# Later adaLN vectors summed in 64 pieces of one feature tile instead of 256 quarters

## Chip, cores and metric

One core of one Trainium2 chip runs the kernel. The metric is the device time of one execution in microseconds (us), from the first to the last work on the core. "SP", "PE", "ACT", "DVE" and "POOL" are the five engines: SP issues most DMAs, PE multiplies matrices, ACT, DVE and POOL do the elementwise work.

## The reference, cut to what matters

One layer of a diffusion block on 256 latent tokens and 256 context tokens of 2048 features, in float32. A conditioning vector is turned into six modulation vectors of 2048 features each (adaLN):

```python
def _modulation(cond, w, bias):
    m = jax.nn.silu(cond) @ w + bias          # w: 2048 x 12288
    return [a[:, None, :] for a in jnp.split(m, 6, axis=-1)]
...
o_c, ctx_states = _mix(_modnorm(h_c, norm1_g[l], m_c[0], m_c[1]), h_c.shape[1], zero, lp)
o_x, _ = _mix(_modnorm(h_x, norm1_g[l], m_x[0], m_x[1]), GRID_W, ctx_states, lp)
h_x = h_x + m_x[2] * o_x
h_x = h_x + m_x[5] * _swiglu(_modnorm(h_x, norm2_g[l], m_x[3], m_x[4]), ffn_w_gu[l], ffn_w_down[l])
```

`_mix` projects the modulated tokens with `w_in` (2048 x some 6800), runs four groups of mixers (GLA, Gated DeltaNet, a short gated convolution, RWKV-7; three of them recurrent in both directions, the context first) and projects with `w_out`. The first two vectors (0 and 1) are needed before any projection. The other four (2 and 5, two gates; 3 and 4, shift and scale of the second norm) are needed only after the mixers. These are "the later vectors".

## The kernel before

The kernel runs in stages. From 0 to 190 us it norms the context tokens, computes vectors 0 and 1 (line 391 loads `ada_w` in tiles `ad` of 1 MB, four column strips of PE sum them into `ada`) and projects some context columns (`acc`). From some 199 to 1190 us it runs the mixers of both token sequences, interleaved with the projections that feed them. Then come the output projection with `w_out`, the second norm, and the SwiGLU, whose weights `w_gu` and `w_down` stream through to the end.

All weights are float32 and are cut into two exact halves: a piece is loaded into `wraw`, `split` copies its upper part to `wh` (ACT, line 156) and subtracts for the rest `wl` (DVE, line 161), and PE multiplies with both. Until the SwiGLU, `wraw` is a ring of six buffers of 128 x 512 (256 KB), and `wh` and `wl` have three each (`wp = [wpool, 512, 3, 6]`: pool, width, halves, raw buffers).

`proj` makes 128 projected columns for all tokens. It goes through the 2048 features in four quarters (`hf`); each loads one `wraw` of `w_in` (SP, line 571), splits it, and sums 12 products into the PSUM bank `big` (line 173 is the helper of all matmuls). This is where the later vectors are fed in: `feed` is a list of steps, and each quarter of a projection takes two steps from its head.

The steps come from `ada_pieces`, for the vectors 3, 4, 2 and 5 in turn: 64 steps `piece(j, kt)` and one `finish` each. A step loads 256 KB of `ada_w` into a buffer of the `wraw` ring (SP, line 255): feature tile `kt` (128 features) and from each of the vector's four groups of 512 columns the quarter `j`, 128 columns. Four matmuls follow, one for each group, with the conditioning `sc` as the weights (128 features x 32, of which two columns are used) and the loaded columns streamed; group `g` goes to partitions 32g to 32g+31 of the one bank `ob`. `finish` takes the sums out of `ob`, through a `wraw` buffer.

The whole program is handed to a scheduler that keeps every engine's queue in an order of priority: an instruction's place in the text, save where `tc.high_priority()` puts loads ahead, or where the list `ORDER` names a piece of mixer work with a number after the colon, by which many instructions the piece is put forward or back. SP's queue runs in order: an issue that waits for a buffer holds up those behind it. In `ORDER`, `XX` loads the latents, `FF` takes the steps that are left in `feed`, `YY` closes the pools in `rws` (the RWKV mixers' tiles) to make room for the mixers' outputs. The columns that a mixer needs later are parked in memory through tiles `xs` and fetched again; `put_y` takes a mixer's output from a tile `y_o` (two buffers), the short convolution's from `sc_y` (two of its own).

Of the kernel before, what the change touches and what calls it, by code (L numbers as in the profile page):

```python
# [13 lines left out]
PSUM = bass.MemoryType.PSUM  # L14
# [21 lines left out]
# Order of the work on the two token sequences, lower case for the context and capitals for the latents:  # L36
# pr, pd, pg project and park the inputs of a mixer; rw, gd, gl run one (RWKV pair, GDN head, GLA pair);
# XX loads the latents and their gates, FF finishes the later adaLN vectors, YY makes room for the mixers'
# outputs on chip, SC is a quarter of the short convolution. After a colon: by how many instructions
# a piece is put forward (or back) against its place.  # L40
# [94 lines left out]
def block_kernel(ctx: ExitStack, tc: tile.TileContext, x, cx, ada_w, ada_b, w_in, w_out, w_gu, w_down,  # L135
# [71 lines left out]
    wp = [wpool, 512, 3, 6]  # L207
# [4 lines left out]
    def split(raw, who, pool=None):  # L212
        """raw = h + l exactly, both of a float32r's width"""
        n = 2 if pool else wp[2]
        h = mk(pool or wp[0], [P, wp[1]], "wh", n, F32R)
        l = mk(pool or wp[0], [P, wp[1]], "wl", n, F32R)
        # wide pieces in two steps, for the products to begin on the first
        n = 2 if wp[1] == 1024 else 1
        w = wp[1] // n
        for i in range(n):  # L220
            sl = slice(i * w, (i + 1) * w)
            acopy(h[:, sl], raw[:, sl])
            tt(l[:, sl], raw[:, sl], h.bitcast(F32)[:, sl], SUB, e=who)
        return h, l

    def logsig(o, zin, tmp, lo=0, hi=P, bias=0.0, badd=None):
        """o = log(sigmoid(zin + bias)); tmp is scratch"""
        act(tmp, zin, AF.Abs, bias=bias)
        act(tmp, tmp, AF.Exp, scale=-1.0)
        act(tmp, tmp, AF.Ln, bias=cst["one"][lo:hi])  # L230
        if badd is None:
            stt(o, zin, 0.0, tmp, MIN, SUB)
        else:
            ts(o, zin, badd, ADD, 0.0, MIN)
            tt(o, o, tmp, SUB)
# [6 lines left out]
    gate_dram = mk(dram, [2, D], "gated")  # L242

    def ada_pieces(ci, bank_of, tmp):
        """adaLN columns of one of the later vectors, in steps to be taken between other work"""
        st = {}

        def piece(j, kt):
            if not st:
                st["ps"] = bank_of([P, 512])  # L250
            ps = st["ps"]
            with tc.high_priority():
                raw = wraw()
                rv = raw.rearrange("p (g c) -> p g c", g=4)
                nc.sync.dma_start(rv, ada_w[kt * P:(kt + 1) * P, ci * D:(ci + 1) * D]
                                  .rearrange("p (g c) -> p g c", g=4)[:, :, j * P:(j + 1) * P])
            for g in range(4):
                mm(ps[32 * g:32 * g + 32, j * P:(j + 1) * P], sc[:, kt, :], rv[:, g], kt == 0, kt == KT - 1)
# [22 lines left out]
        return [lambda j=j, kt=kt: piece(j, kt) for j in range(4) for kt in range(KT)] + [finish]  # L281
# [12 lines left out]
    def open_bank(flat):  # L294
        """zeros in a PSUM bank, left open for sums in any order"""
        n = flat.shape[-1]
        mm(flat, zb[:, :P], zb[:, 0:1].to_broadcast([P, n]), True, False)
        return lambda: mm(flat, zb[:, :P], zb[:, 0:1].to_broadcast([P, n]), False, True)
# [3 lines left out]
    C = mk(kp, [P, NCONST], "consts")  # L302
    sw = mk(kp, [P, 1536], "sw")

    def cc(name, n=P):
        return C[:, COFF[name]:COFF[name] + n]

# [9 lines left out]
    # block-diagonal tiles: off-diagonal blocks stay zero  # L317
# [27 lines left out]
    with ExitStack() as st:  # L345
# [41 lines left out]
        def first_vectors(kt):  # L387
            """modulation of feature tile kt, and the modulated context tokens"""
# [52 lines left out]
        for i, dst in ((0, C), (1, sw)):  # L441
            nc.sync.dma_start(dst, (consts, small)[i])
# [20 lines left out]
    def col_products(ps, wh, wl, a, first, last):  # L463
        """ps[:, 0] + ps[:, 1] += w @ a, w and a in exact halves"""
        both = [lambda: mm(ps, wh, a, first, last), lambda: mm(ps[:, 0], wl, a[:, 0], False, False)]
        for f in both[::-1] if last else both:
            f()

    def row_products(acc, aH, aL, wh, wl, first, last, j):
        """acc[j] += a @ w for one half of the tokens; a is stored transposed, both in exact halves"""  # L470
        ah, al = aH[:, j * P:(j + 1) * P], aL[:, j * P:(j + 1) * P]
        mm(acc[j], ah, wh, first, False)
        mm(acc[j], ah, wl, False, False)
        mm(acc[j], al, wh, False, last)

    # ================= mixers =================
    Y = mk(dram, [16, P, T], "Yd")
    with mix:
# [4 lines left out]
        def runsum(o, i, d, z):  # L483
            """running sums, forward or backward, starting anew where z is zero"""
# [12 lines left out]
        # recurrent states at the end of the context, parked  # L497
# [17 lines left out]
        def PB(shape, tag="e"):  # L515
            """a PSUM bank: two for projections, three for either stream of mixers"""
# [3 lines left out]
        def token_scale(ss, tag, tmp):  # L520
            """ss[j]: partial sums of the squares of a token's features -> the norm's factors, [any, tokens]"""
# [40 lines left out]
        def proj(nHL, segs):  # L562
            """w_in columns of segs, transposed: [columns, tokens] in PSUM"""
            H, L = nHL
            ps = PB([P, T], "big")
            for hf in range(4):
# [7 lines left out]
                for f in feed[:2]:  # L574
                    f()
                del feed[:2]
# [14 lines left out]
        def spill(nHL, name, i, s=1):  # L591
            """project columns and park them"""
# [14 lines left out]
        def sigmoid(o):  # L607
            """o = sigmoid(o), o not under -87"""
# [4 lines left out]
        def silu_to(o, z, tag):  # L613
            """o = z * sigmoid(z)"""
# [5 lines left out]
        def inverse(nL, levels, lowers, rhs=None, out=None, w=P):  # L620
            """(I - nL)^-1 for four unit-triangular matrices; lowers says of each if it is a lower one.
            Diagonal blocks of 16 by substitution, then blocks of doubled size.
            With rhs: out = the inverses' transposes times rhs, instead."""
# [5 lines left out]
            # diagonal blocks, one row per partition  # L629
# [5 lines left out]
            # rows r and 15 - r of a block hold 15 entries together; side by side, the second one backwards  # L635
# [8 lines left out]
            # all entries of a block on every partition of that block  # L644
# [7 lines left out]
            for st in range(15):  # L652
                step = []
                for low, us in groups.items():
                    # the entries (i, j) of all j, i the row that is done
# [61 lines left out]
        def smalls(sm):  # L717
            """gate inputs of low rank, and what hangs on them alone"""
            cur[0] = "b"
            # rows 0..15: inputs of the GLA gate; 32..39: running sums of the GDN log decay;  # L720
            # 64..127: shifted RWKV inputs
# [6 lines left out]
            for d in range(2):  # L728
# [7 lines left out]
                # tanh(z) = 2 sigmoid(2 z) - 1  # L736
# [6 lines left out]
            # Gated DeltaNet: log decay, its running sums, beta  # L743
# [4 lines left out]
            # softplus(z) = -logsig(-z)  # L748
# [22 lines left out]
            # sums over whole chunks, on every partition  # L771
# [3 lines left out]
            esel = C[32:40, COFF["esel"]:COFF["esel"] + 32].rearrange("p (r c) -> p r c", c=4)  # L775
            et = mk(mx, [P, 8, 4], "get", 1)
            # rows 0..3 (forward) use the running sum, rows 4..7 (backward) the reversed one
# [19 lines left out]
        def rw_gates(p, d, sm):  # L797
            """sums of sigmoid(.) inside each chunk of 64 (the log decay over -RW_S), and a"""
# [21 lines left out]
        def halves(dst, src, eng):  # L820
            """src [P, 4, 64] -> the diagonal blocks of dst [P, 4, 2, 64]"""
# [18 lines left out]
        def rwkv(p, s, raw, sm):  # L840
# [6 lines left out]
            for d in range(2):  # L847
# [52 lines left out]
                # values, token-major  # L900
# [5 lines left out]
                # L and M  # L906
# [9 lines left out]
                # decayed keys, token-major  # L916
# [5 lines left out]
                # [nB | nA^T]  # L922
# [9 lines left out]
                # [K~ | A_rk^T], token-major  # L932
# [31 lines left out]
                for n, c in enumerate(order):  # L964
                    # [outputs | state]
# [37 lines left out]
        def conv(o, z, taps, s):  # L1003
            """three-tap convolution along rows of 256 (context) or 64 tokens"""
# [9 lines left out]
        def gdn(h, s, raw, sm):  # L1014
# [40 lines left out]
            # decays between tokens; index d * 2 + c  # L1055
# [57 lines left out]
            for d in range(2):  # L1113
                S = get_state(("gd", h, d), f"gd_S{d}") if s == 1 else None
                for n, c in enumerate((0, 1) if d == 0 else (1, 0)):
                    u = d * 2 + c
                    # [outputs | state]
# [33 lines left out]
        def gla(p, s, raw, sm):  # L1151
# [28 lines left out]
            for d in range(2):  # L1180
# [52 lines left out]
                for n, c in enumerate((0, 1, 2, 3) if d == 0 else (3, 2, 1, 0)):  # L1233
                    # [outputs | state]
# [30 lines left out]
        def short_conv(t, nHL):  # L1265
# [6 lines left out]
            yo = t1("sc_y", 2)  # L1272
# [42 lines left out]
        bdE = Ring(rings, "bdE", [P, 4, 2, 64], 1)  # L1315
        for ci in (3, 4, 2, 5):
            feed += ada_pieces(ci, lambda shape: mk(pb, shape, "ob", 1), mx)
# [111 lines left out]
    # ================= SwiGLU =================  # L1429
# [5 lines left out]
    for f in range(FT):  # L1435
        # sums of the products with the tokens' upper parts, and with their lower ones
        pg = [mk(ps2, [P, 2, T], "acc", 8) for _ in range(2)]
        for k0, nk, bufs in ((0, 8, wide), (8, 4, narrow), (12, 4, narrow)) if f == 0 else ((0, 8, wide), (8, 8, wide)):
# [9 lines left out]
            # the first tile takes the tokens as they get ready  # L1448
# [16 lines left out]
    # the table of the last norm's functions, ahead of it  # L1465
# [7 lines left out]
    for b in range(4):  # L1473
# [3 lines left out]
        for k2 in range(FT // 2):  # L1477
            # the last weights of all are kept for the halves of the tokens in turn
# [32 lines left out]
def prepare(inputs):  # L1511
    """host side: arrays as the launch takes them"""
# [24 lines left out]
```

## Time and profile before

| | us |
|---|---|
| median of 3 runs (lowest, highest) | 2065.49 (2064.67, 2066.31) |
| span of the profiled execution | 2059.4 |
| PE busy in that span | 1933.2 (94%) |
| DVE busy, ACT busy | 1341.9 (65%), 988.3 (48%) |
| the later vectors' products (`ob`), PE busy | 110.4 in 2048 records |

The span goes from the first to the last instruction on the core; the runs' median is 6.1 us over it, for what lies around. Matmuls are pipelined and overlap, so the mean duration of one is longer than the time it adds. "Granted clock" is the share of full speed that PE's clock was given. Every float32 matmul shows as two records.

### The profile page before, as it was taken

What the parts mean: (1) busy time and instruction counts of PE and PEld (TensorE: products, weight loads), DVE (VectorE), ACT (ScalarE), POOL (GpSimd) and SP (SyncE); (2) the same over time, 40 slices, a digit from 0 to 9 for tenths busy, and PEclk for the clock granted to TensorE, in tenths of its full rate; (3) what the DMA queues carried; (4) which work ended last, traced back from release to release, by engine and by line L of the source; (5) the groups of instructions that cost most, each with busy time, mean ns of one, the idle gap of its engine ahead of it and who ended that gap; (6) DMA issues with size and microseconds to landing.
All of it is one profiled execution on the core that took longest, in us unless ns stands there. A gap on an engine that the chain in (4) does not pass through costs nothing.

```text
span 2059.4 us, 37523 instructions
## 1 busy us (share of the span) xinstructions
PE 1933.2 (94%) x13864; PEld 1640.5 (80%) x13864; DVE 1341.9 (65%) x3488; ACT 988.3 (48%) x2013; POOL 163.3 (8%) x210
## 2 busy tenths in 40 slices
PE   4777999979999999999999999899999999999998
PEld 2556787758887887888989978788888888888886
DVE  3333875788778957889897776655555555545554
ACT  2112644564456435555654565555555555544444
POOL 0000100000101000101010000200000000000000
PEclk9899999989999999999999999999999999999999
DMA  9997858834847748534333655466666666665554
GB/s 271 277 275 222 240 162 236 228 103 125 227 139 199 204 140 246 136 82 111 102 105 107 166 186 193 135 187 188 187 185 185 188 188 186 185 234 195 193 195 154
DMA packets 609272, 374.31 MB, mean 182 GB/s; under 512 B 31776, under 2 KB 570784, under 8 KB 608192
## 3 DMA queue, kind: packets, MB, share of 16 engines
q1 hardware_dynamic: 604176, 366.59, 61.3%
q10 hardware_dynamic: 4320, 3.15, 0.5%
q8 instruction: 109, 1.79, 0.4%
q0 software_dynamic: 592, 2.18, 0.3%
q14 instruction: 75, 0.61, 0.1%
HBM read 359.89 MB, written 11.94 MB: 181 GB/s over the span
## 4 chain that ended last, share of the span: by engine, by line
PE 73%; DMA 11%; DVE 8%; issue 3%; ACT 2%; POOL 1%; SPq 0%; ACTq 0%; DVEq 0%; POOLq 0%
PE acc L173 36%; PE big L173 14%; PE la L173 8%; DMA ad<-in_ada_w 6%; PE ea L173 4%; PE lb L173 4%; PE ob L173 3%; PE eb L173 3%; DVE wl L161 2%; DMA wraw<-in_w_in 2%; DMA wraw<-in_ada_w 1%; ACT wh L156 1%; DMA wr<-in_w_in 1%; DVE ivaXc L161 1%; DVE ivaw L161 1%
## 5 line engine op out<-in xcount | busy, mean ns | idle before, releaser
L161 DVE TENSOR_TENSOR wl<-wraw,wh 128x512 fp32r<-128x512 f32 x856 | 568.3, 690 | 417.8 <-ACT wh L156 410.0
L156 ACT ACTIVATE wh<-wraw 128x512 fp32r<-128x512 f32 x856 | 509.9, 625 | 544.6 <-PE acc L173 186.2
L173 PE MATMUL acc<-n,wh 128*128 128x512 f32 x1408 | 493.4, 399 | 3.0 <-ACT wh L156 3.0
L173 PE MATMUL acc<-n,wl 128*128 128x256 f32 x1408 | 382.7, 282 | 0.3 <-DVE wl L161 0.3
L173 PE MATMUL big<-nh,wh 128*128 128x256 f32 x1056 | 319.5, 303 | 0.9 <-ACT xs L156 0.9
L173 PE MATMUL big<-nl,wh 128*128 128x256 f32 x1056 | 308.2, 292 | 0.0
L173 PE MATMUL big<-nh,wl 128*128 128x256 f32 x1056 | 306.7, 291 | 1.2 <-DVE wl L161 1.2
L173 PEld LDWEIGHTS acc<-n,wh 128*128 128x128 f32 x1408 | 259.9, 189 | 59.9 <-ACT wh L156 3.3
L173 PEld LDWEIGHTS acc<-n,wl 128*128 128x128 f32 x1408 | 266.9, 190 | 9.3 <-DVE wl L161 0.8
L173 PEld LDWEIGHTS big<-nh,wh 128*128 128x128 f32 x1056 | 199.7, 189 | 29.6 <-issue 23.5
L173 PEld LDWEIGHTS big<-nh,wl 128*128 128x128 f32 x1056 | 199.9, 190 | 8.1 <-issue 5.2
L173 PEld LDWEIGHTS big<-nl,wh 128*128 128x128 f32 x1056 | 199.9, 189 | 7.3 <-issue 6.7
L173 PE MATMUL acc<-wl,hH 128*128 128x512 f32 x352 | 137.1, 389 | 0.0
L173 PE MATMUL acc<-wh,hH 128*128 128x512 f32 x352 | 137.0, 389 | 0.0
L173 PE MATMUL acc<-wh,hL 128*128 128x512 f32 x352 | 137.0, 389 | 0.0
L173 PE MATMUL ob<-wraw,sc 128*32 128x128 f32 x2048 | 110.4, 284 | 10.7 <-DMA wraw<-in_ada_w 7.0
L173 PEld LDWEIGHTS ob<-wraw,sc 128*32 128x32 f32 x2048 | 52.1, 109 | 45.4 <-DMA wraw<-in_ada_w 12.1
L173 PE MATMUL ada<-ad,sc 128*32 128x256 f32 x512 | 46.0, 510 | 37.6 <-DMA ad<-in_ada_w 35.5
L161 POOL TENSOR_TENSOR hL<-sg,hH 128x256 fp32r<-128x256 f32 x44 | 44.5, 1012 | 453.4 <-ACT hH L156 453.4
L173 PEld LDWEIGHTS acc<-wl,hH 128*128 128x128 f32 x352 | 66.1, 188 | 14.2 <-DVE wl L161 0.2
L173 PEld LDWEIGHTS acc<-wh,hH 128*128 128x128 f32 x352 | 66.1, 188 | 13.7
L173 PEld LDWEIGHTS acc<-wh,hL 128*128 128x128 f32 x352 | 66.1, 188 | 13.6
(473 smaller groups left out, 3130.6 us busy)
## 6 DMA issues: line engine op xcount, KB each, us to landing
wraw<-in_w_gu SPq DMA_DIRECT2D x174, 512.0 KB, 4.0
wraw<-in_w_in SPq DMA_DIRECT2D x260, 256.0 KB, 3.0
wraw<-in_ada_w SPq DMA_DIRECT2D x256, 256.0 KB, 3.7
wraw<-in_w_down SPq DMA_DIRECT2D x88, 512.0 KB, 4.3
ad<-in_ada_w SPq DMA_DIRECT2D x32, 1024.0 KB, 8.4
wraw<-in_w_out SPq DMA_DIRECT2D x64, 256.0 KB, 3.2
wr<-in_w_in SPq DMA_DIRECT2D x32, 256.0 KB, 4.0
xin<-in_cx SPq DMA_DIRECT2D x2, 1024.0 KB
```

Of the source, the lines that this page charges most:

```text
L156: A.activation(o, i, AF.Copy)
L161: (e or V).tensor_tensor(out=o, in0=a, in1=b, op=op)
L173: return TE.matmul(o, l, r, start=start, stop=stop)
```

## The change

A step of the later vectors is now a whole feature tile: `piece(kt)` loads 128 features x 2048 columns of a vector (1 MB, rows of 8 KB) into a tile `araw` of its own with one buffer, and four matmuls of 512 columns, one per group, sum it into the same bank. 64 steps and four `finish` in place of 256 and four. A projection takes one step in every second quarter (`hf % 2 == 0`) in place of two in each, the same number of bytes per projection. `araw` lies in `rws`, behind the RWKV mixers' rings. To make room, the `wraw` ring has four buffers in place of six, the constants leave out the identity (which is held elsewhere too), and the short convolution's outputs share the two buffers `y_o`. `ORDER` with its numbers is unchanged. Comments are taken out (not shown).

```diff
-    wp = [wpool, 512, 3, 6]
+    wp = [wpool, 512, 3, 4]
...
+    araw = [None]
+
     def ada_pieces(ci, bank_of, tmp):
         st = {}
 
-        def piece(j, kt):
+        def piece(kt):
             if not st:
                 st["ps"] = bank_of([P, 512])
             ps = st["ps"]
             with tc.high_priority():
-                raw = wraw()
-                rv = raw.rearrange("p (g c) -> p g c", g=4)
-                nc.sync.dma_start(rv, ada_w[kt * P:(kt + 1) * P, ci * D:(ci + 1) * D]
-                                  .rearrange("p (g c) -> p g c", g=4)[:, :, j * P:(j + 1) * P])
+                raw = mk(araw[0], [P, D], "araw", 1)
+                nc.sync.dma_start(raw, ada_w[kt * P:(kt + 1) * P, ci * D:(ci + 1) * D])
             for g in range(4):
-                mm(ps[32 * g:32 * g + 32, j * P:(j + 1) * P], sc[:, kt, :], rv[:, g], kt == 0, kt == KT - 1)
+                mm(ps[32 * g:32 * g + 32, :], sc[:, kt, :], raw[:, g * 512:(g + 1) * 512], kt == 0, kt == KT - 1)
...
-        return [lambda j=j, kt=kt: piece(j, kt) for j in range(4) for kt in range(KT)] + [finish]
+        return [lambda kt=kt: piece(kt) for kt in range(KT)] + [finish]
...
-    C = mk(kp, [P, NCONST], "consts")
+    C = mk(kp, [P, NCONST - P], "consts")
...
-            nc.sync.dma_start(dst, (consts, small)[i])
+            nc.sync.dma_start(dst, (consts[:, P:], small)[i])
...
                     wh, wl = split(raw, V)
-                for f in feed[:2]:
-                    f()
-                del feed[:2]
+                if hf % 2 == 0:
+                    for f in feed[:1]:
+                        f()
+                    del feed[:1]
...
-            yo = t1("sc_y", 2)
+            yo = t1("y_o", 2)
...
         bdE = Ring(rings, "bdE", [P, 4, 2, 64], 1)
+        araw[0] = rws.enter_context(tc.tile_pool(name="araw", bufs=1, reuse_waits="tile"))
         for ci in (3, 4, 2, 5):
             feed += ada_pieces(ci, lambda shape: mk(pb, shape, "ob", 1), mx)
```

## Rows read from the trace of the kernel before

**Rows 1.** The page: span, and the chain that ended last, by engine and by line.

```profile
span 2059.4 us, 37523 instructions
...
PE 73%; DMA 11%; DVE 8%; issue 3%; ACT 2%; POOL 1%; SPq 0%; ACTq 0%; DVEq 0%; POOLq 0%
PE acc L173 36%; PE big L173 14%; PE la L173 8%; DMA ad<-in_ada_w 6%; PE ea L173 4%; PE lb L173 4%; PE ob L173 3%; PE eb L173 3%; DVE wl L161 2%; DMA wraw<-in_w_in 2%; DMA wraw<-in_ada_w 1%; ACT wh L156 1%; DMA wr<-in_w_in 1%; DVE ivaXc L161 1%; DVE ivaw L161 1%
```

**Rows 2.** Windows: busy us (instructions) of each engine, granted clock, DMA share, GB/s.

```profile
199.00:809.00 610.00, 581.03 (x5482) 475.14 (x5486) 462.98 (x1527) 301.32 (x656) 47.90 (x76) 0.98 0.66 187
...
1700.00:2050.00 350.00, 349.60 (x1679) 293.30 (x1678) 187.63 (x301) 165.72 (x312) 21.09 (x18) 1.00 0.60 192
```

**Rows 3.** Windows for tile `ob` alone: PE, PEld, DVE, ACT; sum over 200 to 850.

```profile
200.00:250.00 50.00, 13.33 (x232) 5.86 (x232) 0.00 (x0) 0.00 (x0) 0.97 0.86 242
...
300.00:350.00 50.00, 11.79 (x228) 5.59 (x220) 0.17 (x1) 0.60 (x1) 1.00 0.84 240
350.00:400.00 50.00, 10.79 (x200) 4.88 (x200) 0.00 (x0) 0.00 (x0) 1.00 0.85 234
...
750.00:800.00 50.00, 11.89 (x240) 5.97 (x240) 0.00 (x0) 0.00 (x0) 1.00 0.82 237
...
sum 650.00, PE 111.31 PEld 52.76 DVE 1.70 ACT 1.20; mean PE 8.56 PEld 4.06 DVE 0.13 ACT 0.09
```

**Rows 4.** Waits between 199 and 812 us: us in total, times, longest.

```profile
ACT wh L156 <- DMA wraw<-in_w_in: 80.6, 55, 4.2
...
PE ob L173 <- DMA wraw<-in_ada_w: 7.0, 12, 2.0
```

**Rows 5.** Timeline of PE, four places: start us, us, engine, line, operation.

```profile
59.91 1.93 PE L173 MATMUL ada<-ad,sc 128*32 128x256 f32 x32 [1.83 <-DMA ad<-in_ada_w]
...
204.47 0.28 PE L173 MATMUL big<-nl,wh 128*128 128x256 f32 x1
204.59 0.27 PE L173 MATMUL big<-nh,wl 128*128 128x256 f32 x1
204.79 0.65 PE L173 MATMUL ob<-wraw,sc 128*32 128x128 f32 x16
205.37 0.39 PE L173 MATMUL big<-nh,wh 128*128 128x256 f32 x1
...
400.21 0.43 PE L173 MATMUL ob<-wraw,sc 128*32 128x128 f32 x8
400.57 0.66 PE L173 MATMUL la<-ivaW,ivaL 128*128 128x64 f32 x4
...
420.02 0.97 PE L173 MATMUL la<-ivaR,consts 128*128 128x480 f32 x2
420.82 0.38 PE L551 MATMUL big<-ident,xs 128*128 128x128 f32 x2
```

**Rows 6.** Timeline of PE: the first and the last quarters with others inside.

```profile
207.81 0.42 PE L173 MATMUL ob<-wraw,sc 128*32 128x128 f32 x6
...
208.79 0.62 PE L173 MATMUL ob<-wraw,sc 128*32 128x128 f32 x10
...
808.15 0.43 PE L173 MATMUL ob<-wraw,sc 128*32 128x128 f32 x8
...
808.94 0.64 PE L173 MATMUL ob<-wraw,sc 128*32 128x128 f32 x14
```

**Rows 7.** DMA issues: count, KB each, median us from issue to landing.

```profile
wraw<-in_ada_w SPq DMA_DIRECT2D x256, 256.0 KB, 3.7
...
ad<-in_ada_w SPq DMA_DIRECT2D x32, 1024.0 KB, 8.4
```

**Rows 8.** Waits of SP's queue over the whole span.

```profile
SPq L255 <- PE ob L173: 140.2, 101, 17.7
```

**Rows 9.** Timeline of SP's queue at the start.

```profile
8.31 3.57 SPq L255 DMA_DIRECT2D wraw<-in_ada_w  x2
11.93 0.50 SPq L364 DMA_DIRECT2D xin<-in_cx  x1
```

More of the change, by code (lines that the diff above doesn't have):

```diff
@@ L301, in block_kernel @@
     kp = mix.enter_context(tc.tile_pool(name="kp", bufs=1, reuse_waits="tile"))
-    C = mk(kp, [P, NCONST], "consts")
+    C = mk(kp, [P, NCONST - P], "consts")
     sw = mk(kp, [P, 1536], "sw")
     def cc(name, n=P):
-        return C[:, COFF[name]:COFF[name] + n]
+        return C[:, COFF[name] - P:COFF[name] - P + n]
     lev = {b: cc(f"lev{b}") for b in LEVS}
@@ L774, in smalls @@
                 V.tensor_copy(er[32:40, d, 0:2], smd[d][32:40, (127 if d == 0 else 0):T:P])
-            esel = C[32:40, COFF["esel"]:COFF["esel"] + 32].rearrange("p (r c) -> p r c", c=4)
+            esel = C[32:40, COFF["esel"] - P:COFF["esel"] - P + 32].rearrange("p (r c) -> p r c", c=4)
             et = mk(mx, [P, 8, 4], "get", 1)
```

## Prediction

> **What bounds the kernel now.** I read the page's head and its chain first [rows 1]: the span is 2059.4 us, and PE work carries most of the chain. The quarters themselves (PE `ob`, 3%, some 62 us) and the loads that they wait for (`wraw<-in_ada_w`, 1%, some 20 us) are a small part, so this change moves tens of microseconds at the very most. The windows come next [rows 2]: between 199 and 809 us, the stretch in which the quarters run, PE is busy 581 of 610 us, so only 29 us of it are plain idle, and the DMA engines are at 0.66. PE's program order is what that stretch lasts on; DMA is near its limit in part of it. The same windows for the tile `ob` alone [rows 3] give the object of the change: 111.3 us of PE in 2048 records. A matmul shows as two records, so a quarter (4 matmuls) is 8 records and 0.435 us. They are unevenly spread: the four densest windows hold 232, 228, 200 and 240 records with the DMA share at 0.82 to 0.86. The waits say that PE itself hardly stands for these loads (7.0 us in 12 times), while ACT waits 80.6 us for `w_in` pieces that come on the same queue [rows 4].
>
> **The products.** What one quarter costs beyond its columns is seen in the order of time [rows 5]. The matmuls of a quarter go to four column strips and run side by side. A single quarter takes from 400.21 to 400.57, 0.36 us; two in a row from 204.79 to 205.37, 0.58 us; so a further quarter costs 0.22 us and each unbroken group some 0.14 us on top. Going in costs as well: the products before follow each other at 0.12 us, the group starts 0.20 us after the last, so 0.08 us per entry. For the new shape the nearest row is `ada`, the same four strips with 256 columns: 32 records in 1.93 us at full clock, 4 groups of four. A new piece is one group of four with 512 columns, as many columns as half of that: 0.96 us. 64 of them are 61.5 us in place of 111.3.
>
> That holds while the four stay together. They often don't: in the timeline I followed the 256 quarters, and they stand in 208 groups with 55 places where other products stand inside a quarter (the first and the last of them, groups of 6 + 10 and of 8 + 14 records, stand in [rows 6]). 42 of the 55 breaks come right after a quarter's first matmul. A broken piece loses the strips' overlap, since a lone matmul streams all its columns by itself. The price of a lone one comes from the 480-column product [rows 5], 420.02 to 420.82: 0.80 us, so 0.85 us for 512 columns, about 1.0 with the group's own 0.14. How many of the new pieces break isn't in the trace. Lower bound: 55 in 256, 14 of 64. Upper bound: breaks follow columns, which stay the same in sum, 55. The breaks after the first matmul come with a slot (two quarters per slot before, one piece after, so at most 42 in 128, 21 of 64), the other 13 with the time that the products take. I take the middle of 14 and 42, 28: 28 us.
>
> So PE for the vectors goes from 111.3 to 61.5 + 28 = 89.5 us, 22 less, and with 92 groups in place of 208 there are 116 x 0.08 = 9 us less of entries: 31 us. All of it is in a stretch where PE is busy throughout, but freed PE time shortens a kernel only where the chain runs over PE. By the chain of the page that is 73%: 23 us.
>
> **The loads.** 256 loads of 256 KB become 64 of 1 MB, rows of 8 KB in place of four runs of 512 B. In the feed stretch 512-byte runs move 187 GB/s at a share of 0.66, 283 GB/s for a full engine set; the `w_down` stage, 2 KB runs, 192 at 0.60, 320 GB/s [rows 2]. 67 MB at 320 in place of 283 are 27 us less of DMA time, which nothing on the chain waits for directly: I count none of it. SP has 192 fewer loads to issue.
>
> What it adds is the wait on a single buffer. Load n+1 is issued when piece n's last matmul is done, so from one piece to the next pass at least a landing and a piece. Landing of 1 MB: below, 256 KB land in 3.7 us [rows 7], of which 0.93 are bytes at 283 GB/s, leaving 2.8, and 1 MB at 320 GB/s takes 3.3, so 6.1 us as an estimate; above, the 1 MB row, 8.4 us, taken with the DMA engines full and two such loads together. The pieces' own spacing: 610/64 = 9.5 us on average, where even 8.4 + 1.0 just fits. In the four dense windows, 900 records are 28 pieces in 200 us, 7.1 us each. 6.1 + 1.0 = 7.1 fits to the hair; 9.4 misses by 2.3 us, 64 us over 28 pieces. I take 0.4 us each, 11 us, near the lower end, because the higher row is one of saturated engines with twice the bytes in flight. The Trainium skill, DMA: Bandwidth & Descriptors, "Anatomy of one DMA", fits a transfer on its software path as 2.0 us plus its bytes at 436 GB/s; that would be an estimate of 4.4 us for this load and no stall at all, so a sum 11 us lower. No row here shows 1 MB as fast, and I don't use it.
>
> Behind the waiting load on SP stand the weights, parked columns and fetches of the mixers. This isn't new: the quarters' issues wait 140.2 us for `ob` now [rows 8]. But the weights have four buffers of their own now, four quarter projections ahead where two were ahead (6 buffers for one weight piece and two quarters). This also covers the loss of two buffers for w_in after the feed and for w_out: a piece lands in 3.7 us, and four quarter projections (12 products of 0.12 us each) take 5.8; w_out's products, with twice the columns, take longer still. I cost it at nothing; without that cover it would be ACT's 80.6 us that grows.
>
> **The start.** Six quarters go out ahead of the norms' work today; two of them hold SP for 3.57 us just before the second load of context tokens [rows 9]. Now weight pieces take those places. Bounds are no gain and 3.6 us; I take 2. The first new piece can only load when the start's buffers are free, at some 200 us, where its predecessors lay ready; a landing (6 us) in which PE has projections to do: nothing.
>
> **Order.** A step is put forward by a count of instructions. A quarter projection with its two quarters had 25, now it has 17.5 on average, so an unchanged offset reaches some 40% further. No row prices this. A bound on either side is a third of the stretch's idle time, 10 us; I take 0. Constants shorter by 64 KB and the short convolution's outputs in the other mixers' two buffers: nothing, both are short and late or early once.
>
> **Sum.** -23 - 2 + 11 = -14 us on the span of 2059.4: 2045.4. The runs' median is 2065.5, 6.1 us over the span (what lies around it); 2045.4 + 6.1 = 2051.5, and 2051 is what I forecast.
>
> **Rivals.**
> *Broken pieces eat it (no change).* With 45 breaks PE gets 61.5 + 45 = 106.5 us, 5 less, entries 99 x 0.08 = 8 less; 13 x 0.73 = 9, 2 from the start, 11 lost on loads: 2065, within 0.2% (4 us, about what a measurement of this kernel can tell from none). For it: 42 of 55 breaks hit the first matmul, which is the one that waits for the load, and every piece now waits for its own. Against: with fewer slots to enter there are fewer places.
> *The single buffer becomes the bound (slower).* Place: the dense windows. If a landing takes over 7.0 us there, 28 x 0.9 = 25 us, the rest of the gain is gone; at 7.3 us the time is 2074, at the 8.4 of the row 2105. For it: DMA shares of 0.82 to 0.86 there, and 0.5 MB of weights on the same queue for each piece. Against: the landing row is of a saturated stage, and mixer products can be put ahead of a piece. The Trainium skill, Trainium Kernel Development and Optimization, "Best Practices", asks for double buffers so that loads overlap compute; by it this case would hold.
> *The shifted order costs (slower):* +10 to +25 with half of the gain lost: 2069 to 2080.
> *All goes well (faster still):* no break, loads hidden: 50 + 144 x 0.08 = 62, x 0.73 = 45, and the chain's 20 us of load waits: 1998.
>
> **Chances and range.** Forecast, with its better side: 0.6 (own range 2025 to 2060). No change 0.16. Single buffer 0.16, order 0.08. The range leaves out the last fifth, half of it at each end: low by some 50 us of the best case's 67, and up to a landing of 7.7 us: 2020 to 2084. Faster by over 0.2% 0.6, within 0.16, slower 0.24.
>
> **What will show it.** `ob` in the windows: some 90 us in 512 records, in about 92 groups; 61 or over 105 would move the sum. The `araw` landing: 6 us or 8. PE's waits for `araw`: over 25 us and the second rival holds. SP's wait for `ob` in 64 places. The stretch's end should move from 809 to about 795 us, and everything behind it keep its length. It would be wrong if that later part changes, by the order or by w_out waiting for its weights.

## The result, and the profile after

The changed kernel takes 2124.89 us (median of 4 runs, 2123.77 to 2131.26) beside 2065.9 us for the kernel before on the same chip: a ratio of 1.0284, 95% interval 1.0265 to 1.0304. It is 2.8% slower, where 2051 us were forecast; the range, to 2084, does not hold it. The profiled execution's span is 2123.7 us. I read it in the order of the prediction. First the page's head and its chain after, against [rows 1]:

```profile
span 2123.7 us, 34088 instructions
...
PE 51%; DVE 5%; ACT 2%; DMA 2%; issue 1%; POOL 1%; ACTq 0%; DVEq 0%; POOLq 0%
```

The chain here is followed over some 62% of the span only, so I don't compare its shares. The object of the change itself, the windows for the tile `ob` (PE, PEld, DVE, ACT busy and counts; clock, DMA share, GB/s), against [rows 3]:

```profile
200.00:300.00 100.00, 11.66 (x72) 1.68 (x72) 0.00 (x0) 0.00 (x0) 0.97 0.61 183
...
400.00:500.00 100.00, 21.90 (x80) 2.62 (x80) 0.00 (x0) 0.00 (x0) 0.80 0.56 171
...
sum 700.00, PE 102.22 PEld 14.93 DVE 1.71 ACT 1.17; mean PE 14.60 PEld 2.13 DVE 0.24 ACT 0.17
```

The products take 102.2 us in place of 111.3, in 512 records. Followed in the order of time they stand in 88 groups, with 24 breaks, 22 of them after a piece's first matmul. That is the picture that was forecast (92 groups, 28 broken), 13 us longer. The last product of a piece starts at 876.5 us, 809.3 before, where about 795 was forecast. The waits between 199 and 900 us (us in total, times, longest), against [rows 4]:

```profile
PEld ob L173 <- DMA araw<-in_ada_w: 23.9, 20, 4.8
PE ob L173 <- DMA araw<-in_ada_w: 18.8, 13, 4.3
...
ACT wh L156 <- DMA wraw<-in_w_in: 6.8, 8, 2.4
```

PE stands 18.8 us for the new loads, 7.0 before; ACT's 80.6 us for `w_in` are down to 6.8. Nothing so far makes 59 us, not even the pieces' late end by itself: the first experiment below has it too (877.0), with most of the loss gone. SP's queue at the start of the feed shows a first loss:

```profile
211.21 7.02 SPq L571 DMA_DIRECT2D wraw<-in_w_in  x4
218.75 0.34 SPq L256 DMA_DIRECT2D araw<-in_ada_w  x1
```

The first piece is issued at 218.75 us, and the first product of a piece starts at 226.1; the first quarter's started at 198.9. But the large loss is 1,000 us later. Windows (all engines) of the last mixers:

```profile
1150.00:1200.00 50.00, 48.30 (x363) 44.75 (x361) 36.94 (x81) 30.15 (x70) 5.45 (x5) 0.97 0.65 169
1200.00:1250.00 50.00, 32.05 (x138) 25.94 (x137) 21.26 (x51) 15.94 (x36) 2.24 (x2) 0.59 0.13 31
1250.00:1300.00 50.00, 48.38 (x277) 41.33 (x276) 25.09 (x40) 22.33 (x38) 0.00 (x0) 1.00 0.72 218
...
1210.00:1240.00 30.00, 19.31 (x64) 14.16 (x64) 10.29 (x28) 8.78 (x21) 1.19 (x1) 0.50 0.00 1
```

Between 1210 and 1240 us the DMA engines stand still, PE runs 64 instructions, and its granted clock is 0.50: the 1.2 GHz level. I call this the hole. SP's queue says what the loads did there, PE's timeline what ended it, and DVE's timeline (rows of `y_o` alone) why:

```profile
1201.17 57.38 SPq L571 DMA_DIRECT2D wraw<-in_w_in  x11
1259.60 1.76 SPq L1378 DMA_DIRECT2D wraw<-in_w_out  x2
```

```profile
1234.93 2.08 PE L173 MATMUL lb<-gd_tok,ones 128*128 128x512 f32 x2 [1.04 <-ACT gd_tok L152]
1241.42 0.58 PE L173 MATMUL big<-nh,wh 128*128 128x256 f32 x1 [4.42 <-DVE y_o L161]
```

```profile
1168.23 0.42 DVE L161 TENSOR_TENSOR y_o<-big,xs 128x256 f32<-128x256 f32 x1
...
1195.85 0.42 DVE L161 TENSOR_TENSOR y_o<-gd_qe,gd_q 128x256 f32<-128x256 f32 x1
...
1198.14 0.42 DVE L161 TENSOR_TENSOR y_o<-gd_qe,gd_q 128x256 f32<-128x256 f32 x1
...
1239.37 0.42 DVE L161 TENSOR_TENSOR y_o<-gd_qe,gd_q 128x256 f32<-128x256 f32 x1
...
1240.62 0.42 DVE L161 TENSOR_TENSOR y_o<-gd_qe,gd_q 128x256 f32<-128x256 f32 x1
1240.95 0.41 DVE L161 TENSOR_TENSOR y_o<-big,xs 128x256 f32<-128x256 f32 x1
```

`y_o<-gd_qe,gd_q` are the outputs of the GLA pairs, `y_o<-big,xs` those of the short convolution. They take turns in two buffers now. The short convolution's second output is behind the last GLA pair's two in that turn, so it is written only at 1240.95, right after them. It reads a bank of `big`; until it has, that bank isn't free, the next projection can't begin, its weights stay in `wh`, `wl` and `wraw`, and SP takes 57 us over eleven loads of `w_in` with the first load of `w_out` behind them. SP's waits in that stretch (1195 to 1262 us) are for buffers whose last reader, the subtraction `wl` on DVE, isn't done:

```profile
SPq L571 <- DVE wl L161: 51.5, 9, 42.3
```

The first load of `w_out` goes out at 1259.6 us, at 1183.5 before: 76 us later, while the first load of `w_gu` is 64 us later (1350.3 beside 1286.4) and the end too (2123.7 beside 2059.4).

### The profile page after: what moved, and what is told of

The parts are those of the page before. It is cut to its first block, busy times and chain, and to the rows that moved or that the text cites. A ratio compares the mean times of both kernels' runs of the same rounds, so it can differ in the third digit from the quotient of the medians.

```text
span 2123.7 us, 34088 instructions
## 1 busy us (share of the span) xinstructions
PE 1956.1 (92%) x12327; PEld 1626.7 (77%) x12328; DVE 1345.0 (63%) x3488; ACT 989.9 (47%) x2013; POOL 160.6 (8%) x210
## 4 chain that ended last, share of the span: by engine, by line
PE 51%; DVE 5%; ACT 2%; DMA 2%; issue 1%; POOL 1%; ACTq 0%; DVEq 0%; POOLq 0%
PE acc L173 34%; PE big L173 7%; PE la L173 3%; PE ea L173 3%; PE lb L173 2%; DVE wl L161 2%; PE eb L173 1%; ACT wh L156 1%; DMA wraw<-in_w_out 1%; DMA wraw<-in_w_in 0%; PE ob L173 0%; DMA araw<-in_ada_w 0%; DVE ivaw L161 0%; DVE ivaXc L161 0%; POOL prt L165 0%
## 5 line engine op out<-in xcount | busy, mean ns | idle before, releaser
L173 PE MATMUL big<-nh,wh 128*128 128x256 f32 x1056 | 314.2, 298 | 13.7 <-DVE y_o L161 4.4
L173 PE MATMUL big<-nh,wl 128*128 128x256 f32 x1056 | 311.6, 296 | 3.3 <-DVE wl L161 3.1
L173 PE MATMUL ob<-araw,sc 128*32 128x512 f32 x512 | 100.6, 640 | 19.0 <-DMA araw<-in_ada_w 18.8
L173 PEld LDWEIGHTS ada<-ad,sc 128*32 128x32 f32 x512 | 21.5, 137 | 50.1 <-issue 46.1
```

The source lines that it names most:

```text
L173: return TE.matmul(o, l, r, start=start, stop=stop)
```

## The experiments

Ratios are to the kernel before on the same chip, with the 95% interval. Each expectation was written before its run and says which theories it weighs; the letters are theirs.

**The shared buffers, undone and alone.** In the changed kernel the short convolution gets two buffers of its own again, in the pool `yp`:

```
-            yo = t1("y_o", 2)
+            yo = mk(yt[2], [P, T], "sc_y", 2)
...
-                    yt += [yH, yL]
+                    yt += [yH, yL, yp]
```

> The changed kernel, with the short convolution's outputs back in two buffers of their own (in the pool that is opened where the mixers' outputs are kept on chip, so that nothing else moves). Theory Y: sharing the two buffers y_o lets the last short convolutions wait for the last GLA pair, whose outputs hold the ring; their projections stand ahead of the output projection, and PE runs the GLA chain alone from 1201 to 1241 us. Then 2075 to 2085 us, no such hole, and the stretch of the vectors' products as long as before this edit. Theory B: the single 1 MB buffer is the loss, and the hole is only where a late feed becomes visible: 2115 to 2125 us.

And the kernel before with that one line of the change:

```
-            yo = t1("sc_y", 2)
+            yo = t1("y_o", 2)
```

> The kernel before, with this one line of the change alone: the short convolution's outputs share y_o. Theory Y: the same hole opens at the end of the mixers, 2095 to 2110 us. Theory B: 2066 us, no change. Between the two, about 2075, if the sharing costs only in the order that the changed feed makes.

The first takes 2087.55 us, 1.0113 (1.0087 to 1.0139), just over what theory Y gave, the second 2106.24, 1.0208 (1.0186 to 1.023), within it. One line costs the kernel before 43 us (2.08% of 2065) and gives back 35 us when it is undone in the changed one (1.71%). DVE's timeline of the first (rows of `sc_y` and `y_o`), and its windows:

```profile
1202.96 0.42 DVE L161 TENSOR_TENSOR sc_y<-big,xs 128x256 f32<-128x256 f32 x1
...
1211.49 0.42 DVE L161 TENSOR_TENSOR sc_y<-big,xs 128x256 f32<-128x256 f32 x1
...
1227.98 0.42 DVE L161 TENSOR_TENSOR sc_y<-big,xs 128x256 f32<-128x256 f32 x1 [0.19 <-PE big L173]
...
1261.09 0.42 DVE L161 TENSOR_TENSOR y_o<-gd_qe,gd_q 128x256 f32<-128x256 f32 x1
```

```profile
1200.00:1250.00 50.00, 48.74 (x325) 43.32 (x325) 33.59 (x65) 26.09 (x51) 2.51 (x2) 0.97 0.65 195
```

Three outputs now pass ahead of the last GLA pair's, PE is full, the clock at 0.97. In the kernel before with the shared buffers the hole is there, without any of the new pieces, and the short convolution's second output comes at 1225.24 us, right behind the last GLA pair's at 1224.91:

```profile
1150.00:1200.00 50.00, 33.55 (x220) 28.70 (x219) 24.78 (x54) 19.49 (x43) 3.98 (x4) 0.77 0.34 88
1200.00:1250.00 50.00, 39.39 (x233) 35.49 (x233) 24.30 (x52) 19.20 (x40) 1.19 (x1) 0.68 0.23 65
```

**The size of the pieces and the ring.** On top of the first experiment: 128 half pieces of 512 KB in two buffers, one in each quarter projection; 256 quarters of 256 KB from four buffers of their own. And the kernel before with a ring of four `wraw` for all. Of the first two only the buffer's line is shown; the slices and the steps per quarter projection change with it.

```
-                raw = mk(araw[0], [P, D], "araw", 1)
+                raw = mk(araw[0], [P, D // 2], "araw", 2)
...
```

> The kernel of e1 with half pieces: 128 of 512 KB (256 columns of each group) in two buffers of half the size, one in every quarter of a projection. The memory is the same, but a load runs while the other half is used. If what is left of the loss in the feed's stretch is the wait on the single buffer, PE's waits for araw (43 us in the changed kernel) fall under 15 us and the time to 2055 to 2065 us. If it is the late first load or the order, it stays within 5 us of e1.

```
-                raw = mk(araw[0], [P, D], "araw", 1)
+                raw = mk(araw[0], [P, 512], "araw", 4)
...
```

> The kernel of e1 with the old 256 quarters, but from four buffers of 256 KB of their own (the same 1 MB of memory) and the weights' ring still at four. If the piece's shape is what costs in the feed's stretch, this is back at 2060 to 2068 us. If it is the own buffer, which can't be loaded before the start's memory is free, and the smaller ring, it stays at e1's 2075 to 2085 us or above, since the quarters' PE time comes back too.

```
-    wp = [wpool, 512, 3, 6]
+    wp = [wpool, 512, 3, 4]
```

> The kernel before with one line of the change alone: the wraw ring of four buffers, which the quarters still share. It bounds what the smaller ring costs. Theory L (the late first load is what is left of the loss): the quarters now have only four buffers with the weights, so some cost, 2070 to 2080 us; more than that and the ring itself has a part in what e1 still loses. No more than 2068 us would clear the ring.

2079.71, 1.0079 (1.0058 to 1.01); 2093.81, 1.0148 (1.0127 to 1.0168); and 2132.14, 1.0306 (1.0269 to 1.0342). So half pieces do help against quarters out of the same memory (for whole pieces, 1.0113, the intervals still overlap), but everything with a separate buffer so far is slower than the kernel before, in which quarters and weights share six buffers. The halves fit neither theory: they aren't back at the kernel before, and the waits for `araw` (PE's and those of its weight loads) are 36 us, not the under 15 expected, beside 43 in the changed kernel. A ring of four that weights and quarters share is the slowest run of all, though its interval overlaps the changed kernel's; in the changed kernel the four serve the weights alone.

**The late first load.** The buffer's memory belongs to the start until some 200 us. It is now taken beside `kp`, ahead of the start, and the residual's gate `g2`, whose place that was, comes into the buffer after the last piece. So with whole pieces, halves and quarters:

```
+    araw[0] = mix.enter_context(tc.tile_pool(name="araw", bufs=1, reuse_waits="tile"))
...
-        araw[0] = rws.enter_context(tc.tile_pool(name="araw", bufs=1, reuse_waits="tile"))
...
-        g2 = mk(yp, [P, D], "g2")
+        g2 = mk(araw[0], [P, D], "araw", 1)
```

> The kernel of e1, but the 1 MB buffer lies in memory that nothing else uses at the start (it is opened with the constants, and holds the first gate vector after the feed), so that the first piece can be loaded before 200 us, as the first quarters were. Theory L: the feed keeps up as before, few pieces fall into the load of the latents, and that load's last tile is fetched at 450 to 460 us in place of 489: 2062 to 2072 us. Theory S (the single 1 MB buffer stalls PE wherever it is): within 5 us of e1's 2088.

> The kernel of e3 (128 half pieces, two buffers of 512 KB) with the buffers opened early as in e6. Theory L: 2055 to 2066 us, since both the late start and some of the waits are gone. Theory S: at e3's 2080 us, as what helped there was the second buffer.

> The kernel of e4 (256 quarters, four buffers of 256 KB of their own) with the buffers opened early. Theory L: 2062 to 2070 us, the kernel before in all but the smaller ring. If it stays at e4's 2094 us, neither the piece's shape nor the late first load explains it, and the own buffers or the ring of four do.

2082.52, 1.0054 (1.0034 to 1.0073); 2079.64, 1.0051 (1.0032 to 1.007); 2092.92, 1.0114 (1.0098 to 1.013). Against the same pieces with the late buffer these are 0.59%, 0.28% and 0.34% less: 12 us for whole pieces, about 6 for the others, where the intervals overlap. So the late load is a part of the loss, and none comes back to the kernel before as theory L had it. With whole pieces the first one starts at 199.9 us in place of 223.4 and the last of the latents' tokens is fetched at 469.6 in place of 489.5, but the last product of a piece isn't earlier (883.0 beside 877.0).

**Pieces that run ahead.** The loads of the latents' tokens, 44 us from first to last issue before (406.9 to 451.0), took 74 in the changed kernel (420.7 to 495.1), with the clock at 0.80 (the window of `ob` from 400 to 500 us above). I took it that pieces go in ahead of the transposes there, and held their products back until the last transpose; also with halves, and with the late buffer:

```
+            with tc.issue_after(hold[0]) if hold[0] else ExitStack():
...
+            hold[0] = tr.ins
```

> The kernel of e6, but the products of the pieces that belong to the latents' projections are placed on PE behind the last transpose of the latents' load, so that none stands inside that load (6 pieces in e6, 5 and a half quarters in the kernel before). Theory D (with a buffer of their own the pieces no longer stand behind the weights in a shared ring, run ahead into the load of the latents, and each holds up its chain of transposes): the load of the latents takes 45 us or less in place of e6's 69, the time falls by 15 to 25 us, to a ratio of 0.993 to 0.999 to the kernel before. Theory S (the single 1 MB buffer stalls PE everywhere): the waits go where the pieces go, within 6 us of e6.

> The same hold on the kernel of e7 (128 half pieces, two buffers of 512 KB). Theory D: the load of the latents at 45 us or less in place of 61, 12 to 20 us less than e7, a ratio of 0.993 to 0.999. Theory S: within 5 us of e7.

> The hold on the kernel of e1, whose first load comes late. Theory D: 10 to 20 us less than e1, a ratio of 1.000 to 1.006, the rest being the late start that e6 showed. If the late start costs only because its pieces spill into the latents' load, this comes out like e9.

2084.39, 1.0106 (1.0079 to 1.0133); 2100.32, 1.0173 (1.014 to 1.0206); 2094.71, 1.0161 (1.013 to 1.0191). The load of the latents did shrink in all three (46 us in place of 69, 41 of 61, 61 of 73), but none is faster than its counterpart, the halves are 1.2% slower. This theory fell: what is gained there is lost later. In the first the last tokens are fetched 25 us sooner, and the first load of `w_out` goes out 4 us later (1214.2 beside 1210.4).

**One half buffer and six of the ring.**

> The kernel of e7 with six wraw buffers again and one buffer of 512 KB in place of two. If the smaller ring of the weights is what e7 still loses (theory R), this gains 8 us or more on e7 in spite of the single buffer. Theory D: the pieces run ahead into the latents' load as before, so within 5 us of e7, or above it by the waits on the single buffer.

2111.52, 1.0236 (1.0211 to 1.0262): 1.9% worse than two half buffers and a ring of four. Two things change at once here, so the run shows only that two more buffers in the ring don't make up for one half buffer less. What the ring of four costs beside a buffer of its own wasn't tried alone.

**Broken pieces.** The early buffer again, with whole pieces and with halves; the last three of a piece's four matmuls are put ahead of other work, so that nothing gets in between. The same line in the kernel before and in the changed kernel as it stands:

```
             for g in range(4):
-                mm(ps[32 * g:32 * g + 32, :], sc[:, kt, :], raw[:, g * 512:(g + 1) * 512], kt == 0, kt == KT - 1)
+                with tc.high_priority() if g else ExitStack():
+                    mm(ps[32 * g:32 * g + 32, :], sc[:, kt, :], raw[:, g * 512:(g + 1) * 512], kt == 0, kt == KT - 1)
```

> The early buffer with whole pieces, and the last three of a piece's four matmuls put ahead of all other PE work, so that nothing stands inside a piece. Theory B (the rest is lost in broken pieces): some 24 broken pieces cost about 1 us each; without them the time falls by 10 to 24 us against the early buffer (2082), to 2058 to 2072. Theory L (the rest is lost because loads of a single 1 MB buffer come late and hold PE or take the DMA engines): no change within 5 us, or a few us more.

> The early buffer with half pieces of 512 KB in two buffers, and the last three matmuls of each kept behind the first. Theory B: some 5 to 15 us less than the early halves (2080), which would bring it to the kernel before or under it. Theory L: within 5 us of 2080, since two buffers still end at 0.5% over before.

> The kernel before with the last three matmuls of each quarter kept behind its first. Theory B (what counts is the time of a broken piece, and the single buffer that it holds): a broken quarter has matmuls of 128 columns, about a quarter of the price of a broken piece, and its buffer is one of six, so 55 breaks give back 5 to 12 us at most: 2053 to 2062. Theory P (keeping pieces together puts the whole of the later work into a better order, whatever the piece): 20 us or more, 2045 or less.

> The changed kernel as it stands, only with the last three matmuls of each piece kept behind its first; the short convolution's shared buffers and the late first load stay. Theory B: its share adds up with the others, 20 to 35 us less than the changed kernel (2125), to 2090 to 2105, and the hole before w_out stays. If the hole in the shared buffers came from the shifted order instead, it would close too: 2070 or less.

No piece is broken in any of the four. Whole pieces: 2051.05 us, 0.9928 (0.9905 to 0.9952), the fastest of all and faster than the kernel before. In its profiled execution, the fastest of the four at 2044.3 us, the first load of `w_out` goes out at 1169.8 us (1183.5 before) and the span is 2042.4. Halves: 2055.8, 0.9949 (0.9926 to 0.9973). The kernel before: 2071.84, 1.0027 (1.0011 to 1.0044). The changed kernel: 2118.47, 1.025 (1.0216 to 1.0284). PE's timeline shows the price of a break, first a broken piece of the early buffer, then a whole one of the kernel with pieces kept together:

```profile
217.63 1.05 PE L173 MATMUL ob<-araw,sc 128*32 128x512 f32 x2
218.61 0.39 PE L173 MATMUL big<-nh,wh 128*128 128x256 f32 x1
...
220.37 1.06 PE L173 MATMUL ob<-araw,sc 128*32 128x512 f32 x6
221.36 0.39 PE L173 MATMUL big<-nl,wh 128*128 128x256 f32 x1
```

```profile
346.93 1.07 PE L173 MATMUL ob<-araw,sc 128*32 128x512 f32 x8
347.92 0.38 PE L173 MATMUL big<-nh,wh 128*128 128x256 f32 x1
```

From its start to the next product's, one matmul alone takes 0.98 us, the other three 0.99, and all four together 0.99 too. A broken piece takes twice as long. The sums of the windows of `ob`: early buffer (32 breaks), pieces kept together, and the kernel before with quarters kept together:

```profile
sum 700.00, PE 110.42 PEld 15.51 DVE 1.72 ACT 1.20; mean PE 15.77 PEld 2.21 DVE 0.25 ACT 0.17
```

```profile
sum 700.00, PE 72.25 PEld 11.03 DVE 1.71 ACT 1.20; mean PE 10.32 PEld 1.57 DVE 0.24 ACT 0.17
```

```profile
sum 700.00, PE 96.38 PEld 46.63 DVE 1.71 ACT 1.20; mean PE 13.77 PEld 6.66 DVE 0.24 ACT 0.17
```

For whole pieces 37 us of PE time go (these windows start at 200 us and miss the first piece of the second sum, about 1 us) and 26 us of the span (1.0054 to 0.9928, 1.26% of 2065). For quarters 15 us of PE time go and none of the span, which is 0.3% longer, as neither theory had it: the line is no help by itself, it belongs to the large pieces. Why the quarters give nothing back isn't settled. In the changed kernel as it stands the line is worth 0.3%, 7 us, with intervals that overlap, far less than the 20 to 35 expected, and the hole stays (clock 0.72 between 1200 and 1250 us). The gains don't add up one by one.

**The loads left out.** The early buffer with whole pieces; 63 of the 64 loads are left out, and all pieces multiply with the first one's columns.

```
-                raw = mk(araw[0], [P, D], "araw", 1)
-                nc.sync.dma_start(raw, ada_w[kt * P:(kt + 1) * P, ci * D:(ci + 1) * D])
+                if len(araw) == 1:
+                    araw.append(mk(araw[0], [P, D], "araw", 1))
+                    nc.sync.dma_start(araw[1], ada_w[kt * P:(kt + 1) * P, ci * D:(ci + 1) * D])
...
```

> The early buffer with whole pieces, but only the first piece is loaded and all 64 pieces multiply with it (so 63 of the 64 loads are left out, and the later adaLN vectors are not the reference's). Theory L: with 63 MB of transfers and all waits for them gone, the time falls under the kernel before, by 30 us or more against the early buffer, to 2050 or less. Theory B, or an order that keeps PE from being filled (theory O): little changes, within 8 us of 2082.

2052.18 us, 0.9937 (0.9918 to 0.9955). That is as much as keeping the pieces together gave, although there are 40 breaks here, in 35 pieces. So breaks aren't the whole cause: leaving the loads out makes up for them. It takes away the waits for a load, SP's waits for the buffer and 63 MB of transfers at once, so which of them counts can't be told from this run. Breaks and loads are tied, since a broken piece holds the only buffer, and the next load waits for it. Waits of SP's queue agree, of the early buffer and of the pieces kept together:

```profile
SPq L256 <- PE ob L173: 123.8, 53, 8.8
```

```profile
SPq L256 <- PE ob L173: 81.0, 46, 7.8
```

The granted clock moves too. Windows (all engines) from 400 to 500 us, of the kernel before, of the early buffer and of the pieces kept together:

```profile
400.00:500.00 100.00, 85.28 (x696) 67.91 (x695) 85.42 (x295) 53.14 (x117) 7.53 (x11) 0.91 0.51 143
```

```profile
400.00:500.00 100.00, 86.13 (x422) 57.96 (x417) 72.31 (x226) 48.39 (x106) 6.14 (x9) 0.78 0.41 128
```

```profile
400.00:500.00 100.00, 85.11 (x594) 68.18 (x593) 86.94 (x295) 54.39 (x117) 6.56 (x11) 0.93 0.48 146
```

PE is busy for about as long in all three, but with the early buffer the clock was 0.78, and 422 PE instructions ran in place of the 594 with the pieces kept together (the kernel before has four times as many for the same bytes of `ada_w`, so its 696 don't compare). With the loads left out the clock there was 0.85. How the 26 us divide between products, loads that come sooner and the clock that goes with both isn't settled; both remedies at once weren't tried.

**The spacing.** The kernel before with four quarters in every second quarter projection, not two in each:

```
-                for f in feed[:2]:
-                    f()
-                del feed[:2]
+                if hf % 2 == 0:
+                    for f in feed[:4]:
+                        f()
+                    del feed[:4]
```

> The kernel before with four quarters in every second quarter projection instead of two in each: the same loads, bytes, ring and products, only bunched as the new pieces are. Theory O (the spacing of the work and the count of instructions that the order's offsets go by are what the rest is): slower by 0.3 to 1%, 2071 to 2086. Theories B and L: within 0.3% of the kernel before.

2099.12 us, 1.0166 (1.0146 to 1.0186): 34 us, over the 1% that the theory of the order gave at most. SP's wait for `ob` grows from 140.2 us [rows 8] to 193.4, so four quarters in a row may take the ring from the weights as well as shift the order; which of the two it is can't be told from this run.

## Why the prediction was wrong

**The step that failed** is "the short convolution's outputs in the other mixers' two buffers: nothing, both are short and late or early once". Short they are, 0.42 us. But a buffer isn't held for the time of its instruction, it is held by the turn in which its users stand. Here a step that was put forward (the short convolution) stood behind one at the end of a long chain (the last GLA pair). Its price is 35 us of the 59 when undone and 43 alone, on top of the mechanism that the step should have followed: `y_o`, `big`, `wh`, `wraw`, SP, `w_out`. The prediction did name the place where it would be seen ("that later part", "w_out waiting for its weights"), but neither as a rival nor with a price. From the first load of `w_gu` on, everything did keep its length: 773.4 us beside 773.0.

**The first piece late: "nothing"** was wrong as well. It costs some 12 us (0.59%). The prediction looked at one landing behind projections; but the first piece started 27 us late (226.1 beside 198.9), and the early buffer brought the latents' tokens 20 us forward. That the last piece's products came no sooner with it leaves open how the 12 us arise.

**Products.** The structure was right: 24 breaks and 88 groups beside 28 and 92, nearly all after the first matmul. (The 28 was taken as the middle of 14 and 42, although the upper bound named was 55.) The sizes were too low: 102.2 us beside 89.5. A whole piece is 72.25 / 64 = 1.13 us on average (0.96 forecast, 0.99 at full clock in the row above); a break costs (102.2 - 75.0) / 24 = 1.13 us more, by the changed kernel with its pieces kept together, not 1.0. A part of it is the clock, which the sum took as full: with the pieces kept together, the 59 that began at a granted clock of 1.00 took 1.07 us each, the five at 0.50 took 1.88.

**Times 0.73.** PE time that is saved doesn't come back at one rate: 26 of 37 us and 21 of 27 (halves, 111.0 to 84.0 us of `ob`, 1.0051 to 0.9949) with the early buffer, 7 of 27 in the changed kernel (102.2 to 75.0), none of 15 in the kernel before.

**Loads.** The landing was 5.1 us in the kernel with pieces kept together, the one of the kernels with whole pieces for which the view of DMA issues has a median (over nine of the 64 loads):

```profile
araw<-in_ada_w SPq DMA_DIRECT2D x64, 1024.0 KB, 5.1
```

The estimate was 6.1. By the Trainium skill, DMA: Bandwidth & Descriptors, "Anatomy of one DMA", whose fit is for the software path, the estimate was 4.4; the row lies between the two. In the changed kernel the 20 pieces for which PE or its weight load waited started 4.5 to 7.7 us after their load's issue, 5.2 in the median. So the landing isn't what made it slow, and the rival of the single buffer doesn't hold as it was put: PE's waits are 18.8 us, under the 25 named, and 11 were in the sum. What the single buffer costs beyond these waits isn't separated: broken pieces hold it longer, and leaving the loads out gave as much as keeping the pieces together. The Trainium skill, Trainium Kernel Development and Optimization, "Best Practices", asks for double buffers. Two half buffers and one whole one come to the same here, 1.0051 and 1.0054, and 0.9949 and 0.9928 with pieces kept together, with intervals that overlap: in the same memory, no gain of a second buffer can be seen.

**The ring: "nothing"** agrees with what can be seen: in the feed ACT's wait for `w_in` fell from 80.6 to 6.8 us, and from the first load of `w_out` to the first of `w_gu` pass 101.5 us with four buffers (pieces kept together, 1169.8 to 1271.3) and 102.9 with six (before, 1183.5 to 1286.4). **The start** gave 1.3 us of the 2 (the first projection at 198.2, at 199.5 before).

**The order: 0, with 10 us on either side.** The bound was too narrow for what spacing can do, as the 34 us of bunched quarters say; what of it acts in the changed kernel isn't known. **The range:** its lower end, 2020, lies 45 us under 2065, not "some 50".

With the shared buffers, the late load and the breaks undone, the pieces give 2051.05 us against 2065.01 on that chip, 14 us. The forecast sum was 14 too, but with breaks and a stall of the loads in it and other sizes, so this is no confirmation of its terms.

## What to carry to other kernels

When a tile moves into another's buffers, ask in which turn the users come, and what the one behind holds meanwhile; a line that looks like saving memory cost most of the time here. A load into a single buffer asks two more things: when its memory first becomes free, and whether the products which read it stay together. A change in several parts should be tried part by part: here a gain of 14 us lay under some 73 us of losses (35, 12 and 26).

## What the runs showed of the hardware

With only a chain of dependent products on PE (19.3 of 30 us busy, 64 instructions), the granted clock was 0.50 between 1210 and 1240 us; before it, with projections back to back, the window's clock was 0.97, and so it was in the same stretch with the short convolution's own buffers. Idle time in PE's feed thus came with slower products, and not only inside the hole: the projection after it still took 0.21 us a product until 1246.7 us, 0.12 from there on. One matmul of 32 rows of output and 512 columns, alone, took as long as four of them in the four strips, 0.98 and 0.99 us: a single other product in between doubles the price.
